# Value projections at 512 moving columns in a decoder trunk: two GLA/stick-breaking mixers re-tiled

## The chip, the cores and the metric

One Trainium2 chip, one core of it. The time is device microseconds (us) of one execution of the whole program; a kernel's time is the median over its runs. The engines are named as in the profile: PE (TensorE matmul), PEld (its weight loads), DVE (VectorE), ACT (ScalarE), POOL (GpSimd), SP (SyncE, which issues the loads of weights).

## The reference

A decoder trunk of two layers on 512 tokens with 1024 features, all in float32. Layer 0 has a gated linear attention (GLA) as its mixer, layer 1 a stick-breaking attention (SB); each mixer stands between two half-step SwiGLU FFNs with 2816 hidden features.

```python
x += 0.5 * swiglu(rmsnorm(x));  x += mixer(rmsnorm(x));  x += 0.5 * swiglu(rmsnorm(x))   # per layer
# GLA: 4 heads, q and k of 128, v and g of 256 features a head
q, k, v, g, gk_lr = split(h @ w_in, [512, 1024, 2048, 3072])
log_a = log_sigmoid(gk_lr @ w_gk2 + b_gk) / 16           # decay of every key feature
o = recurrence(q, k, v, cumsum(log_a))                    # causal, state 128 x 256 a head
out = (rmsnorm(o per head) * silu(g)) @ w_out
# SB: 16 heads of 64 features
q, k, v = split(h @ w_in, 3)
z = q k^T / 8;  w = exp(log_sigmoid(z) - (sum of softplus(z) over later s)), s < t
out = (w @ v) @ w_out
```

The values v are `h @ w_in[:, 1024:2048]` in GLA and `h @ w_in[:, 2048:3072]` in SB. Those two projections are what the change touches.

## The kernel before

All activations stay in the core's memory; every weight is streamed once. A product in float32 accuracy is made of three fp32r matmuls: high part times high part, high times low and low times high. So each weight block is cut by a cast to its high part (`wh`, ACT) and a subtraction to its low part (`wl`, DVE).

**The weight stream.** `Feed` holds a queue of `Entry` objects in the order of use. An entry consists of units (parts of a chunk, 4 KB a partition) and a body, a generator that issues its matmuls and yields after each part; one such part is called a step. A `Chunk` is one load from memory by SP's queue (usually 1 MB). `feed.start()` opens the next entry: it splits the units of up to three entries, so long as no more than four units are held (the pool of `wh` and `wl` has four buffers each), and asks for the loads of up to six. `feed.step(n)` advances by n steps.

**The projections.** `feat` makes 128 features on the partitions with all 512 tokens moving: 24 matmuls of 128x512 in two steps of 12 (`ps_f` in the profile). `tok` makes the values, with tokens on the partitions and weight columns moving (`ps_t`): a call covers 256 columns; for each of four token tiles it issues 24 matmuls of 128x256 into half a PSUM bank, then yields. After every second tile ACT evacuates both halves, each scaled by its tokens' 1/rms (`evac_v`, L691 in GLA and L980 in SB). There are four calls in each mixer, 16 steps, 384 matmuls. PSUM's banks go by tags; tag "a", used by `feat` and `tok` here, has two banks.

**GLA.** `run` first opens the queries, keys, values and gates in the queue. Per head, `levels(h)` builds the decayed score matrix block by block, and `output(h)` transposes keys (`ps_kd`), makes the states (`ps_s`) and the output (`ps_o`), squares it (`osq`), sums over features (`ps_on`), takes 1/rms by the exp and ln tables of ACT (`y`, `vv`) and scales (`on`, L885). A step of the weight stream is put after almost every piece, so that PE has products to do while ACT and DVE work on the chain. At the fourth head the rest of the projections is done, `silu` applies the gates' activation on ACT, and `close` multiplies `on` with the gate and cuts it into `oh` and `ol` for the output projection `back` (`ps_b`).

```python
for n, _ in enumerate(self.levels(h)):
    feed.step(1)
    if prev is not None and n >= 1:
        next(prev, None)          # a part of the previous head's output
        if n == 4:
            feed.step(1)
```

**SB.** The queue holds eight pairs of heads (`pair`: one `feat` for q, one for k) with the four `tok` calls between them. A loop over s = 0..16 makes for head s the logits and their scan (`weights_log`: `ps_z`, softplus on ACT, scan on DVE) and for head s - 1 the weights, transposed (`weights`: `ps_T`, `wt`), and after a pair of heads `values` (`ps_oT`). A list gives the steps of the weight stream for each s.

Of the kernel before, what the change touches and what calls it, by code (L numbers as in the profile page):

```python
# [10 lines left out]
F32 = mybir.dt.float32  # L11
# [19 lines left out]
def decoder(ctx: ExitStack, tc: tile.TileContext, a: dict, out: bass.AP):  # L31
    nc = tc.nc

    # ---------------------------------------------------------------- pools
# [16 lines left out]
    # ------------------------------------------------------------ constants  # L51
# [15 lines left out]
    # --------------------------------------------------------- weight stream  # L67
    # Every weight matrix passes through here in the order of use: chunks of 1 MB are
    # loaded, cut into units of 4 KB a partition, split into high and low parts, and
    # multiplied. An entry is one or more units with the products that use them.  # L70
    class Chunk:
        def __init__(self, src, n, m):
            self.src, self.n, self.m, self.t = src, n, m, None
            self.pool = None
            self.few = False
# [12 lines left out]
    class Entry:  # L88
        """units: (chunk, view of it, n, m); body(W) yields between parts of the products."""

        def __init__(self, units, body):
            self.units, self.body, self.W = units, body, None

        def split(self):
            if self.W is None:
                self.W = []
                for ch, view, n, m in self.units:
                    r = view(ch.load())
                    few = n * m < 1024
                    pool, x, bufs = (st["few"], "v", 1) if few else (wp, "w", 4)  # L100
                    h = pool.tile([P, n, m], F32R, tag=x + "h", bufs=bufs, name="wh")
                    l = pool.tile([P, n, m], F32R, tag=x + "l", bufs=bufs, name="wl")
                    st["cut"] = nc.scalar.copy(h, r).ins  # L103
                    with tc.issue_after(st["gains"]):
                        nc.vector.tensor_tensor(out=l, in0=r, in1=h.bitcast(F32), op=ALU.subtract)  # L105
                    self.W.append((h, l))

    class Feed:
# [3 lines left out]
        def start(self):  # L112
            i = self.pos
            self.pos += 1
            used = 0
            for e in self.q[i : i + 3]:
                used += sum(n * m >= 1024 for _, _, n, m in e.units)
                if used > 4:
                    break
                e.split()  # L120
            for e in self.q[i : i + 6]:
                for u in e.units:
                    u[0].load()
            e = self.q[i]
            return e.body(e.W)

# [26 lines left out]
    def feat(ch, f, evac, tag=None, defer=None):  # L153
        """features f*128.. of a [P, KD, 256] chunk on partitions, all tokens"""
# [16 lines left out]
    def tok(w, c0, evac, tag=None):  # L171
        """columns c0..c0+256 with the tokens on partitions; evac(i, ps[P, 256])"""
        ch = Chunk(cols(w, c0, 256), KD, 256)

        def body(W):
            ps = None
            for i in range(NT):
                if i % 2 == 0:
                    ps = psum("ps_t", tag)
                o = ps[:, (i % 2) * 256 : (i % 2) * 256 + 256]  # L180
                s = slice(i * P, (i + 1) * P)
                for k in range(KD):
# [9 lines left out]
        feed.q.append(  # L192
            Entry([(ch, (lambda t, u=u: t[:, u * 4 : u * 4 + 4]), 4, 256) for u in range(2)], body)
        )
# [66 lines left out]
    def down(w, r0, nf, hs, part, nxt):  # L261
        """x[d] += 0.5 * sum_f w[r0 + f, d] h[f] for the 8 / nf blocks d of a part"""
# [22 lines left out]
    def back_tok(w, r0, nf, hs, done):  # L285
        """the same with tokens on partitions: done(dh, i, ps) gets 512 features of token tile i"""
# [23 lines left out]
    # ----------------------------------------------------------------- norms  # L310
# [24 lines left out]
    def stats_a(tag=None):  # L335
        """r4[token, tile]: 1 / rms of the residual"""
# [23 lines left out]
    def stats_b(tag=None):  # L360
        """R[any partition, token]: the same along the free axis"""
# [11 lines left out]
    def two_halves(between=None):  # L373
        """the next two entries, the first half of both before the second"""
# [20 lines left out]
    def act(o, i, fn, **kw):  # L395
        """an activation of the Exp and Ln tables, queued behind their load"""
        with tc.issue_after(st["tab"]):
            st["last"] = nc.scalar.activation(o, i, fn, **kw).ins

    # ------------------------------------------------------------------- FFN  # L400
    class FFN:
        """The chunks of 256 features go in groups: gate and up, with down for the group
        before between them. From product NORMED on the input is scaled by 1/rms ahead of
        it. The gate's products from chunk SEVEN on, and those of up for the chunks SEVEN_UP,
        go by Winograd's form of Strassen's scheme: seven products of half size for the
        2 x 2 halves of features, inputs and tokens."""
# [5 lines left out]
        def __init__(self, wg, wu, wd, gi, nxt, first=False, last=False):  # L412
# [6 lines left out]
            for group, (c0, c1) in enumerate(self.GROUPS):  # L419
                slots, put = 2 * (c1 - c0), 0  # L420
                for i in range(slots):
# [5 lines left out]
                    if first and c == 0:  # L427
                        # the first products wait for no more of the weights than they need
# [16 lines left out]
                    # the sums are made of the residual as it came  # L445
# [112 lines left out]
        def t_half(self, i, j):  # L558
            """T(i + 1) of input block j"""
# [17 lines left out]
        def normed_input(self):  # L577
            """the scaled input, and T1 = B12 - B11, T2 = B22 - T1, T3 = B22 - B12, T4 = B21 - T2"""
# [21 lines left out]
        def sums(self):  # L600
            def piece(i):
                # in the place of the unscaled input
# [50 lines left out]
    # ------------------------------------------------------------------- GLA  # L653
    class GLA:
        def __init__(self, w_in, w_gk2, b_gk, og, w_out, nxt):
# [13 lines left out]
            for c in range(4):  # L669
                tok(w_in, 1024 + c * 256, lambda i, ps, c=c: self.evac_v(c, i, ps), "a")  # L670
# [235 lines left out]
        def run(self):  # L906
            with ExitStack() as es:
# [20 lines left out]
                for h in range(4):  # L928
# [363 lines left out]
```

## Time and profile before

| | |
|---|---|
| time, median of 3 runs | 1913.95 us (1913.91 to 1914.23) |
| span of the profiled execution | 1913.4 us (it has no time of its own beside it) |
| instructions | 28787 |
| DVE 76%, ACT 49% | 1462.7 us and 943.6 us busy |
| data moved | 179.05 MB, mean 94 GB/s |
| GLA mixer in the trace | about 360 to 595 us |
| SB mixer in the trace | about 1306 to 1554 us |
| 768 value matmuls (ps_t) | 5% of the chain that ended last |

The page gives the busy time of each engine and its share of the span; matmuls are pipelined, so PE's spans overlap and the distance from start to start tells what one costs. The chain of waits is followed back from the last instruction: it tells what released each piece of work. The timeline gives start, duration and, in brackets, the idle time ahead of an instruction and what ended it.

### The profile page before, as it was taken

Reading aid. Unit: us, or ns where it says so; the run is one execution under the profiler, and the core shown is the slowest. Engines: PE = TensorE matmul, PEld = TensorE weight load, DVE = VectorE, ACT = ScalarE, POOL = GpSimd, SP = SyncE. Lnnn points to the kernel's source line nnn. Section 1 sums busy time; section 2 is a strip of 40 time slices with the busy share of each in tenths; the row PEclk is TensorE's granted clock in tenths of the full one; section 3 lists DMA queues with packets and bytes.
Section 4 is the critical chain, followed back from the end, with each engine's and each line's share of the span. In section 5 each row is a group of like instructions: output and inputs, shape, how many; then the busy total and the mean of one; then the engine's idle time right before and its main releaser. Section 6 shows DMA issues by size and latency. Waiting matters only on the chain.

```text
span 1913.4 us, 28787 instructions
## 1 busy us (share of the span) xinstructions
PE 1893.6 (99%) x11789; PEld 1687.9 (88%) x11789; DVE 1462.7 (76%) x2314; ACT 943.6 (49%) x1450; POOL 6.8 (0%) x16
## 2 busy tenths in 40 slices
PE   8999999999999999999999999999999999999998
PEld 7999999889887899999989999998888788899997
DVE  7978777775666977877788778776877779777775
ACT  6534434443554544444453444445878745344444
POOL 0000000100000000000000000000000000000000
PEclk9999999999999999999999999999999999999999
DMA  5423332312123223332233333223221123333321
GB/s 156 144 89 108 103 111 90 96 46 65 60 73 110 89 89 112 105 114 78 78 113 119 100 101 108 79 89 100 66 67 59 63 89 110 99 100 105 116 78 66
DMA packets 177511, 179.05 MB, mean 94 GB/s; under 512 B 3906, under 2 KB 167924, under 8 KB 177380
## 3 DMA queue, kind: packets, MB, share of 16 engines
q1 hardware_dynamic: 176912, 176.24, 29.3%
q8 instruction: 92, 1.51, 0.3%
q0 software_dynamic: 368, 0.95, 0.2%
q14 instruction: 39, 0.32, 0.1%
q10 hardware_dynamic: 100, 0.03, 0.0%
HBM read 175.11 MB, written 2.10 MB: 93 GB/s over the span
## 4 chain that ended last, share of the span: by engine, by line
PE 96%; DVE 2%; DMA 1%; ACT 1%; issue 0%; POOL 0%; SPq 0%; DVEq 0%; POOLq 0%; ACTq 0%
PE ps_d L60 24%; PE ps_f L60 20%; PE ps_w L487 15%; PE ps_z L487 10%; PE ps_q L487 10%; PE ps_t L60 5%; PE ps_b L60 3%; PE ps_S L60 1%; PE ps_z L1019 1%; PE ps_bt L60 1%; PE ps_oT L1081 1%; PE ps_T L1066 1%; PE ps_o L60 1%; DMA x<-in_x_dram 0%; DMA raw<-in_ffn_w_up_dram 0%; DVE wl L105 0%
## 5 line engine op out<-in xcount | busy, mean ns | idle before, releaser
L105 DVE TENSOR_TENSOR wl<-raw,wh 128x1024 fp32r<-128x1024 f32 x244 | 261.4, 1072 | 94.7 <-ACT wh L103 72.8
L103 ACT CAST wh<-raw 128x1024 fp32r<-128x1024 f32 x244 | 226.0, 931 | 142.3 <-PE ps_f L60 44.5
L60 PE MATMUL ps_d<-hh,wh 128*128 128x512 f32 x672 | 262.9, 391 | 0.0
L60 PE MATMUL ps_d<-hh,wl 128*128 128x512 f32 x672 | 262.7, 391 | 0.0
L60 PE MATMUL ps_d<-hl,wh 128*128 128x512 f32 x672 | 262.3, 390 | 0.0
L103 ACT CAST wh<-s 128x1024 fp32r<-128x1024 f32 x136 | 142.7, 1049 | 153.9 <-PE ps_q L487 84.1
L276 DVE SCALAR_TENSOR_TENSOR x<-ps_d,x 128x512 f32<-128x512 f32 x184 | 126.0, 688 | 101.1 <-PE ps_d L60 100.7
L105 DVE TENSOR_TENSOR wl<-s,wh 128x1024 fp32r<-128x1024 f32 x136 | 166.4, 1223 | 32.4 <-ACT wh L103 27.4
L60 PE MATMUL ps_f<-xh,wh 128*128 128x512 f32 x448 | 182.1, 407 | 2.9 <-DVE q L682 1.5
L60 PE MATMUL ps_f<-xl,wh 128*128 128x512 f32 x448 | 175.4, 392 | 0.0
L60 PE MATMUL ps_f<-xh,wl 128*128 128x512 f32 x448 | 175.0, 391 | 0.0
L103 ACT CAST wh<-rawd 128x1024 fp32r<-128x1024 f32 x84 | 88.4, 1052 | 160.1 <-PE ps_d L60 139.2
L487 PE MATMUL ps_z<-th,wl 128*128 128x256 f32 x544 | 154.0, 283 | 0.0
L487 PE MATMUL ps_z<-th,wh 128*128 128x256 f32 x544 | 154.0, 283 | 0.0
L487 PE MATMUL ps_z<-tl,wh 128*128 128x256 f32 x544 | 153.9, 283 | 0.0
L487 PE MATMUL ps_w<-nl,wh 128*128 128x256 f32 x544 | 153.6, 282 | 0.0
L487 PE MATMUL ps_w<-nh,wl 128*128 128x256 f32 x544 | 153.4, 282 | 0.0
L487 PE MATMUL ps_w<-nh,wh 128*128 128x256 f32 x544 | 153.4, 282 | 0.0
L60 PEld LDWEIGHTS ps_d<-hl,wh 128*128 128x128 f32 x672 | 126.1, 188 | 27.6
L60 PEld LDWEIGHTS ps_d<-hh,wh 128*128 128x128 f32 x672 | 126.3, 188 | 25.5
L60 PEld LDWEIGHTS ps_d<-hh,wl 128*128 128x128 f32 x672 | 126.3, 188 | 24.9
L105 DVE TENSOR_TENSOR wl<-rawd,wh 128x1024 fp32r<-128x1024 f32 x84 | 102.9, 1225 | 46.3 <-ACT wh L103 33.4
(246 smaller groups left out, 4725.3 us busy)
## 6 DMA issues: line engine op xcount, KB each, us to landing
raw<-in_ffn_w_gate_dram SPq DMA_DIRECT2D x43, 1024.0 KB, 5.4
raw<-in_ffn_w_up_dram SPq DMA_DIRECT2D x43, 1024.0 KB, 5.3
rawd<-in_ffn_w_down_dram SPq DMA_DIRECT2D x84, 512.0 KB, 3.5
raw<-in_gla_w_in_dram SPq DMA_DIRECT2D x12, 1024.0 KB, 5.3
raw<-in_sb_w_in_dram SPq DMA_DIRECT2D x16, 512.0 KB, 3.9
raw<-in_gla_w_out_dram SPq DMA_DIRECT2D x4, 1024.0 KB, 5.0
raw<-in_sb_w_in_dram SPq DMA_DIRECT2D x4, 1024.0 KB, 5.1
raw<-in_sb_w_out_dram SPq DMA_DIRECT2D x4, 1024.0 KB, 5.1
```

Of the source, the lines that this page charges most:

```text
L60: nc.tensor.matmul(ps, l, r, start=first, stop=last)
L103: st["cut"] = nc.scalar.copy(h, r).ins
L105: nc.vector.tensor_tensor(out=l, in0=r, in1=h.bitcast(F32), op=ALU.subtract)
L276: nc.vector.scalar_tensor_tensor(out=xs[k], in0=ps, scalar=0.5, in1=xs[k], op0=ALU.mult, op1=ALU.add)
L487: nc.tensor.matmul(o, l_, r_, start=first and j + n == 0, stop=j == 3 and n == 2, skip_group_check=True)
L1019: nc.tensor.matmul(o_, l_, r_, start=first, stop=last, skip_group_check=True)
L1066: nc.tensor.transpose(ps[:, c0 : c0 + P], ys[yb][:, yc + j * P : yc + (j + 1) * P], ident)
L1081: nc.tensor.matmul(po[e * 64 : e * 64 + 64, j * P : T], self.v[j][:, c : c + 64], self.wt[p, e][bk][:, c0 : c0 + n], start=j == 0, stop=j ...
```

## The change

`tok` covers 512 columns a call, in two calls for each mixer. Its weights are four units of 2 blocks x 512 columns (two chunks of 4 blocks x 512, 1 MB each). The four token tiles go in two pairs; a pair holds two PSUM banks, walks the four units, and yields after each unit: 12 matmuls of 128x512 a step, 8 steps a call, 16 steps a mixer as before. Each tile is evacuated by one instruction of 128x512 at the pair's last unit. `Entry.split` can ready a part of an entry's units, `Feed.start` hands out what is left of the four, `ahead` readies one more unit at each step of the second pair, and `loads` asks for loads while no more than two chunks of a kind are unsplit.

Around it, GLA makes its additional step in the second head also at n = 3, so that one step less is left for the fourth. In SB the values' second half comes after pair 4 (it was in four quarters after pairs 0, 2, 4 and 6), six steps are made ahead of the loop instead of four, and the first two heads get two steps each instead of three. FFNs are not edited.

```diff
     def tok(w, c0, evac, tag=None):
-        ch = Chunk(cols(w, c0, 256), KD, 256)
+        units = []
+        for k0 in range(0, KD, 4):
+            ch = Chunk(w[k0 * P : k0 * P + 512, c0 : c0 + 512].rearrange("(k p) c -> p k c", p=P), 4, 512)
+            for u in range(0, 4, 2):
+                units.append((ch, (lambda t, u=u: t[:, u : u + 2]), 2, 512))
         def body(W):
-            ps = None
-            for i in range(NT):
-                if i % 2 == 0:
-                    ps = psum("ps_t", tag)
-                o = ps[:, (i % 2) * 256 : (i % 2) * 256 + 256]
-                s = slice(i * P, (i + 1) * P)
-                for k in range(KD):
-                    wh, wl = W[k // 4]
-                    mm(o, st["h"][k][:, s], wh[:, k % 4], k == 0, False)
-                    mm(o, st["h"][k][:, s], wl[:, k % 4], False, False)
-                    mm(o, st["l"][k][:, s], wh[:, k % 4], False, k == KD - 1)
-                if i % 2:
-                    evac(i - 1, ps[:, 0:256])
-                    evac(i, o)
-                yield
+            for pair in ((0, 1), (2, 3)):
+                ps = [psum("ps_t", tag) for _ in pair]
+                for u in range(4):
+                    wh, wl = W[u]
+                    for n, i in enumerate(pair):
+                        s = slice(i * P, (i + 1) * P)
+                        for kk in range(2):
+                            k = 2 * u + kk
+                            mm(ps[n], st["h"][k][:, s], wh[:, kk], k == 0, False)
+                            mm(ps[n], st["h"][k][:, s], wl[:, kk], False, False)
+                            mm(ps[n], st["l"][k][:, s], wh[:, kk], False, k == KD - 1)
+                        if u == 3:
+                            evac(i, ps[n])
+                    if pair[0]:
+                        feed.ahead()
+                    yield
...
 class Feed, start():
             for e in self.q[i : i + 3]:
-                used += sum(n * m >= 1024 for _, _, n, m in e.units)
-                if used > 4:
+                n = sum(n * m >= 1024 for _, _, n, m in e.units)
+                e.split(4 - used if n else 1)
+                used += n
+                if used >= 4 and n:
                     break
-                e.split()
-            for e in self.q[i : i + 6]:
-                for u in e.units:
-                    u[0].load()
+            self.loads(i)
...
+        def ahead(self):
+            for e in self.q[self.pos : self.pos + 4]:
+                if not e.whole():
+                    e.split(1)
+                    self.loads(self.pos)
+                    return
...
 class GLA:
-            for c in range(4):
-                tok(w_in, 1024 + c * 256, lambda i, ps, c=c: self.evac_v(c, i, ps), "a")
+            for c in range(2):
+                tok(w_in, 1024 + c * 512, lambda i, ps, c=c: self.evac_v(c, i, ps), "a")
...
-                            if n == 4:
+                            if n == 4 or n == 3 and h == 1:
                                 feed.step(1)
...
 class SB:
-            pair(0), vals(0), pair(1), pair(2), vals(1), pair(3), pair(4), vals(2)
-            pair(5), pair(6), vals(3), pair(7)
+            pair(0), vals(0), pair(1), pair(2), pair(3), pair(4), vals(1)
+            pair(5), pair(6), pair(7)
...
-                feed.step(4)
-                steps = [3] * 12 + [2, 1, 1, 2, 2]
+                feed.step(6)
+                steps = [2, 2] + [3] * 10 + [2, 1, 1, 2, 2]
```

More of the change, by code (lines that the diff above doesn't have):

```diff
@@ L73, in __init__ @@
             self.src, self.n, self.m, self.t = src, n, m, None
+            self.left = 0
             self.pool = None
@@ L91, in __init__, with whole, split @@
         def __init__(self, units, body):
[L92 to L106, printed above, removed]
+            self.units, self.body, self.W = units, body, []
+            for u in units:
+                u[0].left += 1
+        def whole(self):
+            return len(self.W) == len(self.units)
+        def split(self, parts=4):
+            for ch, view, n, m in self.units[len(self.W) :][:parts]:
+                r = view(ch.load())
+                ch.left -= 1
+                few = n * m < 1024
+                pool, x, bufs = (st["few"], "v", 1) if few else (wp, "w", 4)
+                h = pool.tile([P, n, m], F32R, tag=x + "h", bufs=bufs, name="wh")
+                l = pool.tile([P, n, m], F32R, tag=x + "l", bufs=bufs, name="wl")
+                st["cut"] = nc.scalar.copy(h, r).ins
+                with tc.issue_after(st["gains"]):
+                    nc.vector.tensor_tensor(out=l, in0=r, in1=h.bitcast(F32), op=ALU.subtract)
+                self.W.append((h, l))
     class Feed:
@@ L116, in start, with loads @@
             for e in self.q[i : i + 3]:
-                used += sum(n * m >= 1024 for _, _, n, m in e.units)
-                if used > 4:
+                n = sum(n * m >= 1024 for _, _, n, m in e.units)
+                e.split(4 - used if n else 1)
+                used += n
+                if used >= 4 and n:
                     break
-                e.split()
-            for e in self.q[i : i + 6]:
-                for u in e.units:
-                    u[0].load()
+            self.loads(i)
             e = self.q[i]
             return e.body(e.W)
+        def loads(self, i):
+            seen, held = set(), {False: 0, True: 0}
+            for e in self.q[i : i + 6]:
+                for ch, _, _, _ in e.units:
+                    if id(ch) in seen:
+                        continue
+                    seen.add(id(ch))
+                    if ch.left and ch.pool is None:
+                        held[ch.few] += 1
+                        if held[ch.few] > 2:
+                            return
+                    ch.load()
+        def ahead(self):
[3 more added lines that the diff above has]
+                    self.loads(self.pos)
+                    return
         def step(self, n=1):
@@ L171, in tok @@
     def tok(w, c0, evac, tag=None):
[L173 to L194 removed]
+        units = []
[3 more added lines that the diff above has]
+                units.append((ch, (lambda t, u=u: t[:, u : u + 2]), 2, 512))
+        def body(W):
+            for pair in ((0, 1), (2, 3)):
[14 more added lines that the diff above has]
+                    yield
+        feed.q.append(Entry(units, body))
     def back(w, r0, nf, hs, scale, nxt, late=0, tags=(None,) * 8):
@@ L691, in evac_v @@
             nc.scalar.activation(
[L692 removed]
+                self.v[i][:, c * 512 : c * 512 + 512], ps, AF.Copy, scale=st["r4"][:, i : i + 1]
             )
```

5 lines of the change are left out of this document (2 added, 3 removed).

## The prediction

> **What bounds the kernel now.** I read the page first: busy shares, clock row, and the shares of the chain that ended last.
>
> ```profile
> PE 1893.6 (99%) x11789; PEld 1687.9 (88%) x11789; DVE 1462.7 (76%) x2314; ACT 943.6 (49%) x1450; POOL 6.8 (0%) x16
> PEclk9999999999999999999999999999999999999999
> PE 96%; DVE 2%; DMA 1%; ACT 1%; issue 0%; POOL 0%; SPq 0%; DVEq 0%; POOLq 0%; ACTq 0%
> ```
>
> TensorE (PE) is busy 99% of the span and 96% of the chain. So time can only come from PE's own work or from its idle time, and the view of waits, PE alone, says how much idle time there is.
>
> ```profile
> PE ps_g L1210 <- DMA gl<-in_gla_o_norm_dram: 5.8, 1, 5.8
> PE ps_f L60 <- DVE q L682: 1.5, 1, 1.5
> PE ps_x L1217 <- DMA x<-in_x_dram: 1.4, 4, 0.7
> PE ps_f L60 <- DVE x L211: 1.4, 1, 1.4
> PE ps_o L60 <- DVE on L885: 0.7, 1, 0.7
> PE ps_b L60 <- ACT oh L902: 0.5, 1, 0.5
> ```
>
> Together 11.3 us, 7.2 of it on the first loads. No wait on a weight's load stands here, and only 0.7 + 0.5 = 1.2 us lie inside the mixers' hand-made weaves (ps_o, ps_b); what else there is are single waits of 0.2. The edit can therefore gain from cheaper matmuls, and lose wherever it takes cover from an ACT or DVE chain. The span is 1913.4 us and the median of the runs 1913.95; the 0.55 us between them I keep constant. The profiled execution has no time of its own beside its span.
>
> **Term 1, the matmuls: a gain.** Half of the columns per matmul becomes full width: 768 of 256 become 384 of 512, that is 32 steps of 24 become 32 steps of 12. The chain of waits, pieces in order (start, us, what), has both widths in both mixers.
>
> ```profile
> 455.56 2.93 PE ps_t L60 x24
> 497.02 2.82 PE ps_f L60 x12
> 1317.36 5.87 PE ps_t L60 x48
> 1329.87 5.47 PE ps_f L60 x24
> 1361.12 2.87 PE ps_t L60 x24
> 1350.00 2.77 PE ps_f L60 x12
> 1837.35 2.82 PE ps_w L487 x24
> 1848.72 5.59 PE ps_d L60 x24
> ```
>
> ps_t is the value projection at 256 columns, ps_f a projection at 512 with the same products. One step surrounded by other work costs 2.93 against 2.82 in GLA and 2.87 against 2.77 in the stick-breaking mixer (SB): 0.10 to 0.11 saved. Two steps in a row give 5.87 against 5.47, 0.20 a step. In the last FFN 24 narrow ones take 2.82 and 12 wide ones 5.59/2 = 2.795: only 0.025. So 32 steps save between 0.8 and 6.4 us. Most steps lie among other work, like the first and third pair of rows, a few follow one another; I take 0.12, 3.8 us.
>
> [...]
>
> **Term 2, the end of GLA: a loss.** The extra step at `n == 3 and h == 1` takes a step of 12 ps_f matmuls from the place before the fourth head's output, where they cover a serial chain. Before, PE ran 30 ps_f after the third ps_on; the changed order has 19 (11 fewer), then three ps_kd, then one ps_o ahead of twelve ps_b. Here is the timeline (start, duration, engine; rows of PE, then ACT, then DVE).
>
> ```profile
> 549.03 1.12 PE L60 MATMUL ps_on<-osq,ones 128*128 128x512 f32 x2
> 557.89 0.50 PE L60 MATMUL ps_b<-oh,wh 128*128 128x512 f32 x1 [0.55 <-ACT oh L902]
> 560.65 1.21 PE L60 MATMUL ps_o<-S,v 128*128 128x128 f32 x6 [0.65 <-DVE on L885]
> ...
> 550.92 0.63 ACT L398 ACTIVATE y<-vv 128x512 f32<-128x512 f32 x1 [2.08 <-DVE vv L871]
> 551.58 1.28 ACT L398 ACT_TABLE_LOAD   x1
> 553.30 0.62 ACT L398 ACTIVATE y<-y 128x512 f32<-128x512 f32 x1
> 555.76 0.61 ACT L878 ACTIVATE y<-y 128x512 f32<-128x512 f32 x1
> 556.28 1.04 ACT L103 CAST wh<-raw 128x1024 fp32r<-128x1024 f32 x1
> 557.23 1.13 ACT L902 CAST oh<-on 128x512 fp32r<-128x512 f32 x2
> ...
> 556.41 0.69 DVE L879 TENSOR_TENSOR vv<-vv,y 128x512 f32<-128x512 f32 x1 [2.43 <-ACT y L878]
> 557.66 0.42 DVE L880 TENSOR_SCALAR vv<-vv 128x512 f32<-128x512 f32 x1
> 557.99 1.22 DVE L105 TENSOR_TENSOR wl<-raw,wh 128x1024 fp32r<-128x1024 f32 x1
> 559.85 1.41 DVE L885 SCALAR_TENSOR_TENSOR on<-ps_o,gT,y 128x512 f32<-128x512 f32 x2
> ```
>
> I walk the changed order with these durations, from ps_on = 0; an engine's next instruction starts some 0.1 before the former's end, as 556.28 does against 555.76 + 0.61. PE: two ps_on 1.12 / 2 = 0.6 ahead of the next start, 19 ps_f at 2.82 / 12 = 0.235, ps_kd: done at 5.4. ACT: y (ln) starts at 1.9 as here, table load until 3.8, y's exp until 4.9, y's square until 5.4, then the cast wh until 6.4. There oh followed; in the changed order the next table load (1.28) and the gate's silu (as wide as y: 0.6) stand behind the cast and are followed by one more load (1.28), so that oh starts at 9.6. DVE: vv by y until 6.1, wl until 7.6 (it waits for wh), vv 0.4, y by vv 0.7, and the two on, done at 9.4 and 10.0. ps_o needs the bank that on reads and starts near 9.4, ps_b with the first oh near 10.1, and its third product waits a little more for ol. PE idles 4.7 us where it idled 1.2: +3.5 us. Bounds: +1.5 if only the shorter cover counts, 11 x 0.235 = 2.6, less the 1.2 that a chain without the load ahead of y's square comes earlier; +4.5 if the second on and all of ol are needed before anything runs. The step itself isn't lost: it runs in the second head, where PE has no wait that it could fill.
>
> **Terms 3 and 4, SB: losses.** Steps of SB are rebalanced: six instead of four run before the scan loop, and the first two heads get 2 each instead of 3. Windows (busy us of PE, PEld, DVE, ACT in turn):
>
> ```profile
> 1317.00:1335.00 18.00, 18.00 (x132) 17.08 (x132) 11.96 (x24) 9.58 (x14) 0.00 (x0) 1.00 0.32 94
> 1335.00:1345.00 10.00, 10.00 (x49) 8.08 (x48) 7.60 (x12) 9.14 (x18) 0.00 (x0) 1.00 0.32 95
> 1345.00:1356.00 11.00, 11.00 (x59) 8.80 (x58) 10.77 (x17) 9.00 (x18) 0.00 (x0) 1.00 0.17 50
> 1381.00:1406.00 25.00, 25.00 (x134) 19.39 (x132) 21.55 (x33) 21.05 (x41) 0.00 (x0) 1.00 0.23 69
> 1481.00:1505.00 24.00, 23.39 (x126) 16.83 (x124) 20.08 (x31) 22.45 (x49) 0.00 (x0) 1.00 0.27 88
> ```
>
> The two heads of the first pair are the second and third rows: 21.0 us of PE over ACT 18.1 and DVE 18.4. Two steps less leave PE 21.0 - 2 x 2.77 = 15.5 us, while ACT keeps nearly all its work, since pair 1's scaling and casts now run there whole, just ahead of their use, where before a pair stood between. PE is then short by at most 18.1 - 15.5 = 2.6 us by ACT and 2.9 by DVE. In front, in the first row, ACT has 8 us of 18 free and takes some of it, the casts of the two steps' units (1.04 each) to begin with: I take 1.7, bounds 0 and 2.9.
>
> Values' second half now lies after pair 4 and before pair 5, so pair 5's K too is made just before use, once, and by one head: half of the above, +0.8 (0 to 1.5). In stretches of projections only (fourth row) ACT and DVE have 4 us of 25 to spare, in the tail (fifth row) ACT has 1.5 of 24 and PE already lost 0.61; that is why such a place costs anything.
>
> **What I cost at nothing.** Evacuations: 32 of 128x256 become 16 of 128x512. From
>
> ```profile
> L691 ACT ACTIVATE v<-ps_t,r 128x256 f32<-128x256 f32 x16 | 6.8, 469 | 9.0 <-PE ps_t L60 8.9
> ```
>
> and 0.63 for a 512-wide ACTIVATE (550.92, above), ACT saves 32 x 0.47 - 16 x 0.63 = 5 us in all; ACT is off the path at those places, so nothing is gained. In exchange a pair of tiles holds both banks of tag "a" until its last step, and the next group waits for both evacuations: 0.63 and 1.26 us behind the last matmul. The other tag's step (2.8 us) usually stands between; if that cover is gone it costs up to 1 us at each of the pairs' ends, four places in GLA, which I keep in the range. Weights: units are cut one ahead at a time in the second pair; a unit serves 24 wide matmuls, over 5 us, its cut is one wh (1.04) and one wl (1.22). The loads on SP's queue keep their order and their bytes, with rows twice as long, and no wait on them stood in the list of waits. FFN keeps its order but for a few exchanged neighbours on DVE. The 1.4 us stall on x L211 shifts along unchanged.
>
> **Sum.** -3.8 + 3.5 + 1.7 + 0.8 = +2.2 us: span 1915.6, time 1916.1 (1913.95 + 2.2).
>
> **Rivals.** (a) The gain comes through: the steps save 0.20 each as the two in a row do, 6.4 us, SB's covers hold (ACT did have 4 us to spare in 25), and GLA's end costs 2.5: -3.9, 1910.0. Against it: single steps showed 0.10. (b) Slower: in the long stretch of projections without values, pairs 2, 3 and 4 come just in time as well, not only 1 and 5. Each costs the mean of 1.7 and 0.8, together +3.8: 1919.9. It decides where the last ps_f of a pair's K ends less than some 2 us (scaling, cast and remainder in series, each about the 0.63 to 0.69 of the 512-wide rows above) before its first ps_z. For it speaks DVE's 21.55 of 25; against it that the loop still gives three steps a head there.
>
> (c) The clock falls in GLA's stall. At the kernel's start, after sparse work, ps_f start 0.42 apart until 18.39 and 0.23 from there, although the clock row above is full; the first one behind the 1.39 us stall lasts 0.50, hardly more than usual.
>
> ```profile
> 17.55 0.63 PE L60 MATMUL ps_f<-xl,wh 128*128 128x512 f32 x1
> 18.39 0.39 PE L60 MATMUL ps_f<-xh,wl 128*128 128x512 f32 x1
> 18.62 0.40 PE L60 MATMUL ps_f<-xl,wh 128*128 128x512 f32 x1
> 612.06 0.50 PE L60 MATMUL ps_f<-xh,wh 128*128 128x512 f32 x1 [1.39 <-DVE x L211]
> ```
>
> My 4.7 us of idle lies between those cases. The start's seven or so slow matmuls at 0.2 extra each cost 1.4 us: 1917.5. [...] No row of this trace tells whether a 4 us stall is enough.
>
> (d) The wide matmuls gain only what the last FFN shows, 0.8: +5.2, 1919.1. (e) The change does not do what it says, the two banks held by a pair making PE wait as much as the width saves: near 1914.
>
> **How the numbers follow.** Forecast 0.44, (a) 0.18, (b) 0.16, (c) 0.10, (d) 0.06, (e) 0.06. About 0.2%, 3.8 us, is what a measurement of this kernel can tell from no change, so the bounds are 1910.1 and 1917.8. Faster: nearly all of (a) and a little of the forecast with its low bounds, 0.18. Slower: (b), (d), a part of (c) and the forecast's upper bounds, 0.31. Same: 0.51. The range reaches from (a)'s 1909.8 to a little beyond (b), 1920.4; the forecast's own, with half of each term's spread, is 1913.5 to 1918.5.
>
> **What would show it.** Right: ps_t 128x512 pieces of 12 at 2.77 to 2.82 in the chain; new PE waits near GLA's end on DVE on and ACT oh of 4 to 5 us together; waits of ps_T, ps_z on ACT wt, kh and DVE kl at SB's first pair and at pair 5. Wrong: GLA's wait under 2 us, PE waits at pairs 2 to 4, waits of ps_t or the next group on the evacuations, or pieces of 12 over 2.9.

## The result, and the profile after

| | before | changed |
|---|---|---|
| time, median of 11 runs | 1914.23 us (1913.91 to 1915.09) | 1918.92 us (1918.08 to 1919.53) |
| ratio | | 1.0023 (95% interval 1.0015 to 1.0032) |
| span of the profiled execution | 1913.4 us | 1916.1 us (its time: 1918.08) |

The change costs 4.7 us, 0.24%, and no run of the changed kernel is as fast as the slowest of before. In every later run of both kernels the time is 1.7 to 2.2 us above the span. So the profiled execution of before, with its span of 1913.4, was one of about 1915.3 us and not one at the median; most of what it has too much lies in the first loads, and the two spans differ by only 2.7 us. The comparison is therefore made stage by stage.

The page, PE's busy time and the chain's shares:

```profile
PE 1892.2 (99%) x11405; PEld 1668.2 (87%) x11405; DVE 1461.4 (76%) x2314; ACT 941.3 (49%) x1434; POOL 6.8 (0%) x16
PE 94%; DVE 3%; ACT 2%; DMA 1%; issue 0%; DVEq 0%; ACTq 0%; SPq 0%
```

PE has 384 instructions less. Its busy share is the same 99%, but its share of the chain falls from 96% to 94%, and DVE's and ACT's rise. The view of waits, PE alone, says where:

```profile
PE ps_o L60 <- DVE on L916: 4.1, 1, 4.1
PE ps_T L1097 <- ACT wt L429: 1.9, 2, 1.4
PE ps_f L60 <- DVE q L713: 1.5, 1, 1.5
PE ps_x L1248 <- DMA x<-in_x_dram: 0.6, 3, 0.3
PE ps_z L1050 <- DVE kl L1037: 0.6, 2, 0.3
PE ps_z L1050 <- DVE kh L1035: 0.3, 1, 0.3
```

Against the same view of before: ps_o waits 4.1 instead of 0.7, ps_b's 0.5 is gone, ps_T, kl and kh are new, and the 1.4 on x at the second FFN's start is missing. The chain of waits has the wide pieces themselves:

```profile
456.25 2.82 PE ps_t L60 x12
1316.54 5.62 PE ps_t L60 x24
1411.25 2.77 PE ps_t L60 x12
```

2.93, 5.87 and 2.87 have become 2.82, 5.62 and 2.77: the width pays 0.10 to 0.13 a step at these places, where the forecast took 0.12. Now the end of GLA. The timeline (start, duration; PE, then ACT, then DVE):

```profile
557.91 0.77 PE L60 MATMUL ps_o<-S,v 128*128 128x128 f32 x2 [4.13 <-DVE on L916]
558.45 0.80 PE L60 MATMUL ps_b<-oh,wh 128*128 128x512 f32 x1
559.04 0.63 PE L60 MATMUL ps_b<-oh,wl 128*128 128x512 f32 x1
559.47 0.63 PE L60 MATMUL ps_b<-ol,wh 128*128 128x512 f32 x1
...
561.69 0.39 PE L60 MATMUL ps_b<-ol,wh 128*128 128x512 f32 x1
...
553.49 1.04 ACT L108 CAST wh<-raw 128x1024 fp32r<-128x1024 f32 x1
554.55 1.28 ACT L925 ACT_TABLE_LOAD   x1
555.85 0.63 ACT L925 ACTIVATE gn<-gn 128x512 f32<-128x512 f32 x1
556.49 1.28 ACT L424 ACT_TABLE_LOAD   x1
557.78 2.18 ACT L933 CAST oh<-on 128x512 fp32r<-128x512 f32 x4
...
554.70 1.22 DVE L110 TENSOR_TENSOR wl<-raw,wh 128x1024 fp32r<-128x1024 f32 x1
557.02 1.41 DVE L916 SCALAR_TENSOR_TENSOR on<-ps_o,gT,y 128x512 f32<-128x512 f32 x2
```

The chain of cast, table load, gate, table load and oh on ACT, and of wl, vv, y and on on DVE, runs as the prediction walked it. Behind the idle time the first products start 0.43 us apart; from 561.47 on it is 0.23 again, and their duration falls from 0.63 to 0.39. The windows around them, with the granted clock as the third number from the end, say why:

```profile
556.00:559.00 3.00, 1.08 (x3) 1.00 (x4) 2.93 (x5) 2.98 (x5) 0.00 (x0) 0.81 0.58 177
559.00:561.00 2.00, 2.00 (x6) 1.53 (x5) 2.00 (x5) 1.33 (x3) 0.00 (x0) 0.50 0.70 267
561.00:563.00 2.00, 2.00 (x10) 1.62 (x9) 1.91 (x4) 1.22 (x2) 0.00 (x0) 0.93 0.00 0
```

The granted clock stands at 0.50 in the middle row. If it is 0.50 or full at any moment, which is an assumption, the three rows make 3.4 us of low clock in all (an estimate). Rival (c) has come about, on top of the forecast. In SB the timeline shows five waits that before does not have, three at the first pair, one at pair 5, one in the tail:

```profile
1355.12 0.44 PE L1097 MATMUL ps_T<-ident,r 128*128 128x128 f32 x2 [0.59 <-ACT wt L429]
1357.66 0.53 PE L1050 MATMUL ps_z<-kh,mq 128*128 128x384 f32 x2 [0.27 <-DVE kh L1035]
1359.92 0.44 PE L1050 MATMUL ps_z<-kl,mq 128*128 128x384 f32 x1 [0.32 <-DVE kl L1037]
1461.12 0.44 PE L1050 MATMUL ps_z<-kl,mq 128*128 128x384 f32 x1 [0.24 <-DVE kl L1037]
1491.12 0.44 PE L1097 MATMUL ps_T<-ident,r 128*128 128x128 f32 x2 [1.36 <-ACT wt L429]
```

Between the starts of PE's rows that bound the stages, each from one profiled execution (us; the last four kernels are experiments below; ps_st and ps_R are the small products that make a block's 1/rms, and each head of GLA has one ps_on, each pair of heads in SB one ps_oT):

| stage | before | changed | e1 | e6 | e10 | e12 |
|---|---|---|---|---|---|---|
| start to GLA's ps_R | 378.95 | 377.70 | 377.53 | 378.17 | 376.85 | 378.21 |
| ps_R to the third ps_on | 170.08 | 170.38 | 168.09 | 168.06 | 168.05 | 168.04 |
| third to fourth ps_on | 31.22 | 32.53 | 32.06 | 33.42 | 33.66 | 31.04 |
| fourth ps_on to the second FFN's ps_st | 37.61 | 36.42 | 36.30 | 36.28 | 36.28 | 36.48 |
| ps_st to SB's ps_R | 705.20 | 704.96 | 704.96 | 705.21 | 704.97 | 704.97 |
| SB's ps_R to the first ps_oT | 44.39 | 45.62 | 45.64 | 44.41 | 44.16 | 43.67 |
| first to last ps_oT | 155.55 | 158.05 | 158.03 | 155.39 | 156.45 | 156.46 |
| rest | 390.40 | 390.44 | 390.39 | 390.46 | 390.48 | 390.43 |

Without the first row, which holds the first loads, changed less before is +0.30 + 1.31 - 1.19 - 0.24 + 1.23 + 2.50 + 0.04 = +3.95 us. The profiled execution of the changed kernel is its fastest; its median lies 0.8 higher.

### The profile page after: what moved, and what is told of

Read it like the earlier page. It is cut to its first block, busy times and chain, and to the rows that moved or that the text cites. A ratio compares the mean times of both kernels' runs of the same rounds, so it can differ in the third digit from the quotient of the medians.

```text
span 1916.1 us, 28001 instructions
## 1 busy us (share of the span) xinstructions
PE 1892.2 (99%) x11405; PEld 1668.2 (87%) x11405; DVE 1461.4 (76%) x2314; ACT 941.3 (49%) x1434; POOL 6.8 (0%) x16
## 3 DMA queue, kind: packets, MB, share of 16 engines
q8 instruction: 89, 1.46, 0.3%
## 4 chain that ended last, share of the span: by engine, by line
PE 94%; DVE 3%; ACT 2%; DMA 1%; issue 0%; DVEq 0%; ACTq 0%; SPq 0%
PE ps_d L60 24%; PE ps_f L60 19%; PE ps_w L518 15%; PE ps_z L518 10%; PE ps_q L518 10%; PE ps_t L60 5%; PE ps_b L60 3%; PE ps_S L60 1%; PE ps_bt L60 1%; PE ps_oT L1112 1%; PE ps_z L1050 1%; PE ps_o L60 1%; PE ps_T L1097 1%; DVE l L1075 1%; ACT l L429 0%; DVE wl L110 0%
```

## The experiments

Theory: the wide products gain about 4 us, GLA's end loses it in idle time and half clock, SB loses as much again at single places of its weave. Main rival: the wide form with its two held banks costs the time itself. "Against before" is always against runs of the kernel before on the same chip.

### e1: who pays for GLA's additional step

```diff
-                            if n == 4 or n == 3 and h == 1:
+                            if n == 4 and h != 2 or n == 3 and h == 1:
```

> The changed kernel, but GLA's additional step at n == 3 of the second head is paid by the third head (its own additional step at n == 4 is left out) and no longer by the end: 30 instead of 19 ps_f again between the third ps_on and ps_kd. My theory (the changed kernel's +4.7 us against before is -4.2 of cheaper matmuls, +2.9 of PE idle at GLA's end, +1.4 of products at half clock behind that idle time, and some +3.5 in SB, less 1.2 at the second FFN's start): the 4.1 us wait of ps_o and the slow ps_b go, 4.3 us; the second FFN's start may wait its 1.2 us for a load again; so +0.4 to +1.6 against before. Rival (the wide matmuls and the two banks that a pair holds cost the time themselves, the place of the step nothing): +4 to +5 as now.

Measured: 1915.46 us against 1913.94, +1.52; ratio 1.0008 (0.9999 to 1.0017). The view of waits:

```profile
PE ps_o L60 <- DVE on L916: 1.5, 1, 1.5
PE ps_b L60 <- ACT oh L933: 0.7, 1, 0.7
PE ps_T L1097 <- ACT wt L429: 2.0, 2, 1.4
```

4.1 has become 1.5 + 0.7, and 3.2 of the 4.7 us are back. By the code the step is needed in the second head (the state products there read values of all four token tiles, which the wide form completes four steps later than quarters did); a kernel without it was not run. The third head can pay for it, the end of the mixer can't. In the table, ps_R to the third ps_on with equal numbers of steps: 170.08 - 168.09 = 2.0 us for 16 wide steps, 0.125 each. The changed kernel has one step more in this stretch, which costs 170.38 - 168.09 = 2.3 us. The wait at the second FFN's start did not return.

### e2: SB's list of steps as before

```diff
-                feed.step(6)
-                steps = [2, 2] + [3] * 10 + [2, 1, 1, 2, 2]
+                feed.step(4)
+                steps = [3] * 12 + [2, 1, 1, 2, 2]
```

> The changed kernel with SB's list of steps as before (four ahead of the loop, three in each of the first two heads); the values keep their new places. My theory: the three waits at the first pair (0.59, 0.27 and 0.32) go, the wait of 1.36 in the tail stays: -1.0 us against the changed kernel, +3.7 against before. Rival (the waits come from the values' places, not the list): within 0.3 of the changed kernel, +4.7.

Measured: 1918.75 us against 1913.94, +4.81; ratio 1.0024 (1.0015 to 1.0033). A miss: the rival was right. Two waits went and others came (ps_z on r 0.9 in three places), and from SB's ps_R to the first ps_oT it takes 45.79 us where the changed kernel takes 45.62. The list is not the cause.

This run's profile also shows a longer stretch of half clock in a GLA that is the same program:

```profile
556.00:559.00 3.00, 1.49 (x4) 1.24 (x5) 2.96 (x5) 2.98 (x6) 0.00 (x0) 0.60 0.78 240
559.00:561.00 2.00, 2.00 (x6) 1.60 (x6) 2.00 (x4) 0.92 (x3) 0.00 (x0) 0.50 0.46 172
561.00:563.00 2.00, 2.00 (x6) 1.51 (x6) 1.92 (x4) 1.22 (x2) 0.00 (x0) 0.50 0.00 0
```

The next window, 563 to 566, still has 0.93, so by the same estimate the clock is low for 6.8 us where it was 3.4 above, and the third to the fourth ps_on takes 33.70 us instead of 32.53. Such a difference, 1.2 us, could be most of the spread of 1.5 us between the changed kernel's runs: the granted clock on record is 0.998 in the five fastest of its eleven runs and 0.997 in four of the six others. Other causes of the spread were not separated.

### e4: the new weave alone, with 256 columns

```diff
 (kernel before)
-            pair(0), vals(0), pair(1), pair(2), vals(1), pair(3), pair(4), vals(2)
-            pair(5), pair(6), vals(3), pair(7)
+            pair(0), vals(0), vals(1), pair(1), pair(2), pair(3), pair(4), vals(2), vals(3)
+            pair(5), pair(6), pair(7)
 (the values' first two calls take banks of tag "z", before only the first)
-                            if n == 4:
+                            if n == 4 or n == 3 and h == 1:
-                feed.step(4)
-                steps = [3] * 12 + [2, 1, 1, 2, 2]
+                feed.step(6)
+                steps = [2, 2] + [3] * 10 + [2, 1, 1, 2, 2]
```

> The kernel before, its value projections in calls of 256 columns, with only the weave of the changed kernel: the additional step at n == 3 of the second head, SB's calls two after pair 0 and two after pair 4, six steps ahead of the loop and two in each of the first two heads. My theory: it pays for the weave without the gain of the width: +4.7 + 4.2, about +9 (+7.5 if a part of the waits shrinks since each narrow step covers 0.13 more). Rival (the weave costs nothing, the wide form does): 0 to +1.

Measured: 1922.62 us against 1913.94, +8.68; ratio 1.0044 (1.0032 to 1.0057). The same waits stand in it:

```profile
PE ps_o L60 <- DVE on L885: 4.1, 1, 4.1
PE ps_T L1066 <- ACT wt L398: 1.4, 1, 1.4
```

So the weave costs 8.7 us with narrow values, and the changed kernel is 8.68 - 4.69 = 4.0 us faster than that. The rival that the wide form costs the time is ruled out. But the 4.0 us are not 0.125 for each of 32 steps. Stage by stage, e4 against the changed kernel, GLA up to the third ps_on takes 172.38 and 170.38 us, 2.0 for its 16 steps; the second FFN's start gives 0.8, which comes from a load (see "At nothing" below) and not from the width; and SB with the FFNs ahead of it takes 705.22 + 46.28 + 158.00 and 704.96 + 45.62 + 158.05, only 0.9 for the other 16. The changed kernel pays about 1 us there at a place that e4 does not have (e9).

### e5: the idle time cut in two

```diff
 (GLA.output, behind vv = 1.5 - 0.5 vv y y)
+            if h == 2:
+                mm(psum("ps_x", "z"), ones, vv, True, True)
```

> The changed kernel with one extra product of 128x512 (ones by vv, the result unused) that becomes ready in the middle of the idle time at GLA's end and cuts the 4.1 us in two. My theory (half clock because PE was idle for some 4 us at one stretch): the granted clock stays at 1.0 there, the twelve ps_b behind it start 0.23 apart instead of 0.43, -1.4 us, so +3.3 against before. Rival (those products are slow because their operand ol comes one by one from DVE): no change of the rate, +4.7 or a little more.

Measured: 1917.17 us against 1913.94, +3.23; ratio 1.0016 (1.0007 to 1.0025). The timeline:

```profile
556.05 1.10 PE L60 MATMUL ps_x<-vv,ones 128*128 128x512 f32 x2 [2.62 <-DVE vv L911]
557.57 0.68 PE L60 MATMUL ps_o<-S,v 128*128 128x128 f32 x4 [0.42 <-DVE on L918]
558.10 0.50 PE L60 MATMUL ps_b<-oh,wh 128*128 128x512 f32 x1
558.44 0.40 PE L60 MATMUL ps_b<-oh,wl 128*128 128x512 f32 x1
```

More work, less time: the products behind the gap last 0.40 and not 0.63, and the third to the fourth ps_on takes 31.07 us, 1.46 less. The granted clock is 1.00 in each window from 553 to 566. They were slow because of the idle time, not because of ol: PE's order is a little different here, with products of oh ahead of those of ol, but e10 has that order too, and with the low clock (0.55 in its window from 557 to 560) they start 0.43 apart in it.

### e6: GLA wide, SB as before

The edit: e1, with SB's four calls of 256 columns, their order and the list of steps from the kernel before.

> GLA as in e1 (512 columns, the step paid by the third head), SB wholly as before (four calls of 256 columns, their places and the list of steps). My theory (losses in SB come from the values' places, and the stages add up): GLA and the second FFN's start keep e1's 236.5 us where before has 238.9, SB returns to before's: -2.5 us against before, 1911.4. Rival (a part of SB's loss is carried into it, or GLA's gain is given back later): +0 to +1.5 like e1.

Measured: 1912.37 us against 1913.84, -1.47; ratio 0.9993 (0.9984 to 1.0001). SB returns to 44.41 and 155.39, so the stages add up, and its losses are made by SB itself. One us of the expected 2.5 is missing, and in the profiled execution a window in GLA shows a place for it, with a granted clock of 0.60:

```profile
557.00:560.00 3.00, 2.28 (x9) 1.71 (x8) 3.00 (x6) 2.99 (x6) 0.00 (x0) 0.60 0.40 78
```

The low clock also stood behind the smaller gaps of 1.5 and 0.7 us, but not in every execution: e1's and e9's profiles, with the same GLA, have a granted clock of 1.00 from 557 to 566 and take 32.06 and 32.05 us from the third to the fourth ps_on, those of e6, e7, e8 and e10 have 0.81 in that stretch and take 33.42 to 33.66.

### e7: pair 1 ahead of the values

```diff
 (e1)
-            pair(0), vals(0), pair(1), pair(2), pair(3), pair(4), vals(1)
+            pair(0), pair(1), vals(0), pair(2), pair(3), pair(4), vals(1)
 (pair 1 takes banks of tag "z", its q is evacuated when R is there; the values take "a")
```

> e1 with pair 1's q and k projected ahead of the values' first half (their banks exchanged with the values'), so that they lie a whole group before their use. My theory (the first pair's waits of 0.60, 0.27 and 0.35 come from K made just before use): they go, -1.2 to -2.0 against e1, -0.5 to +0.3 against before. Rival (ACT and DVE are short of time in the first two heads whatever the order): the waits stay in another form, within 0.4 of e1.

Measured: 1913.64 us against 1913.84, -0.20; ratio 1.0000 (0.9991 to 1.0008). The three waits of the first pair are gone; in its list ps_T and kl keep one wait each, those of the tail and of pair 5:

```profile
PE ps_T L1097 <- ACT wt L429: 1.4, 1, 1.4
PE ps_z L1050 <- DVE kl L1037: 0.2, 1, 0.2
```

From the first ps_z to the first ps_oT 26.45 us instead of e1's 28.42, 2.0 less. So what hurt was that all eight steps of values lie ahead of pair 1, whose K is then made just before use.

### e8: the second half in quarters

```diff
 (e1; quarter(c) is the narrow call of before)
-            pair(0), vals(0), pair(1), pair(2), pair(3), pair(4), vals(1)
-            pair(5), pair(6), pair(7)
+            pair(0), vals(0), pair(1), pair(2), pair(3), pair(4), quarter(2)
+            pair(5), pair(6), quarter(3), pair(7)
```

> e1 with the values' first half at 512 columns and the second half in two calls of 256, after pairs 4 and 6, as before. My theory (the wait of 1.36 in the tail, the cut ps_oT and the late kl come from pairs 5, 6 and 7 standing in a row at the end, since the whole second half lies ahead of them): from the first to the last ps_oT 155.5 to 155.8 us as before, not 158.0: -2.3 against e1, -0.8 against before. Rival (the tail's wait is a delay handed on from the first pair): 1.36 stays, within 0.5 of e1.

Measured: 1913.12 us against 1913.84, -0.72; ratio 0.9996 (0.9987 to 1.0005). From the first to the last ps_oT 155.88 us, not 158.03, and the wait of 1.36 is gone, though the waits at the first pair are as in e1. The tail's wait is therefore its own, and it comes from the place and not from the width, as e4 has 1.36 there with narrow values: with quarter(3) between pairs 6 and 7, ACT and DVE get four steps without casts of q and k.

### e9: the second half after pair 5

```diff
 (e1)
-            pair(0), vals(0), pair(1), pair(2), pair(3), pair(4), vals(1)
-            pair(5), pair(6), pair(7)
+            pair(0), vals(0), pair(1), pair(2), pair(3), pair(4), pair(5), vals(1)
+            pair(6), pair(7)
```

> e1 with the values' second half, 512 columns, after pair 5 instead of pair 4. My theory: pair 5's late kl (0.22) and the cut ps_oT between pairs 3 and 5 go, which gives 0.8 to 1.3, the tail's wait of 1.36 stays as pairs 6 and 7 still stand in a row: +0.2 to +0.8 against before. Rival (the values are then late for pair 4's ps_oT, since they end only one head ahead of it): a new wait there, +1.5 or more.

Measured: 1913.35 us against 1913.84, -0.49; ratio 0.9997 (0.9989 to 1.0006), a miss on the good side of +0.2 to +0.8. First to last ps_oT 156.34 us, 1.7 less than e1, with a wait of 1.5 in the tail as foreseen. Between the third and the fifth ps_oT it takes 24.48 + 24.48 us, e1 21.73 + 29.08: there the changed order cuts pair 3's ps_oT in two with a step between, as in this timeline of the changed kernel:

```profile
1439.08 1.07 PE L1112 MATMUL ps_oT<-wt,w 128*64 128x512 f32 x2
1440.08 0.50 PE L60 MATMUL ps_f<-xh,wh 128*128 128x512 f32 x1
...
1443.07 2.37 PE L1112 MATMUL ps_oT<-wt,w 128*64 128x512 f32 x14
```

1.00 + 2.30 us to the next start, where the uncut sixteen take 1419.65 - 1417.35 = 2.30 at the pair before in the same trace: about 1 us without any idle time in the list of waits. e4, which does not cut it, takes 25.04 + 25.10 us over the same twelve steps, less than the changed kernel's 21.73 + 29.11 although five of them are narrow. An edit that moves the cut alone was not tried.

### e10: both moves together

The edit: e7's and e9's orders in one kernel, all values wide.

> e7 and e9 together: all values at 512 columns, the step paid by GLA's third head, pair 1 ahead of the values' first half, the second half after pair 5. My theory (SB's losses are single places and add up): from ps_R of SB to the last ps_oT 17.2 + 26.5 + 156.3 = 200.0 us, as before has 199.9 and e1 203.7; GLA keeps e1's gain, less what half clock takes in some executions; -1.5 against before, as e6. Rival (the moves exclude each other, a wait goes from one place to the next): 202 us and more, +0.5.

Measured: 1911.76 us against 1913.89, -2.13; ratio 0.9990 (0.9982 to 0.9999). SB takes 44.16 + 156.45 = 200.6 us; e1 203.7, before 199.9. The moves add up; of the waits that before does not have, SB keeps the tail's, 1.5, and 0.3 at the first pair.

### e11: still more cover at GLA's end

```diff
 (e6)
-                            if n == 4 and h != 2 or n == 3 and h == 1:
+                            if n == 4 and h < 2 or n == 3 and h == 1:
```

> e6 (GLA at 512 columns, SB as before) with the fourth head's additional step left out as well: 42 ps_f between the third ps_on and ps_kd instead of 30. My theory (what is left to lose in GLA is PE's idle time of 1.5 + 0.7 us at its end, and half clock behind it in some executions): the wait of ps_o falls below 1 us, the granted clock stays at 1.0, the heads before lose nothing; -1.9 against e6, -3.3 against before. Rival (the step was cover in the fourth head, its chain then waits there): new waits between the heads' ps_kd and ps_on of 1 us and more, -1.5 or worse.

Measured: 1912.17 us against 1913.89, -1.72; ratio 0.9990 (0.9981 to 0.9999). A miss: 0.25 better than e6 where 1.9 was expected. One line of waits and the timeline of ACT:

```profile
PE ps_b L60 <- ACT oh L958: 2.4, 1, 2.4
...
553.29 1.05 ACT L108 CAST wh<-raw 128x1024 fp32r<-128x1024 f32 x1 [2.44 <-PE ps_f L60]
554.24 0.63 ACT L950 ACTIVATE gn<-gn 128x512 f32<-128x512 f32 x1
554.87 1.28 ACT L449 ACT_TABLE_LOAD   x1
556.16 2.18 ACT L958 CAST oh<-on 128x512 fp32r<-128x512 f32 x4
```

ps_o no longer waits, but ps_b does. The steps put there make the last gate, and oh stands behind that gate's activation and a table load on ACT: the cover moves the end of the chain it is to cover. This execution, the second fastest of eleven, has the full clock behind the 2.4 us (1.00 in each window from 557 to 566); the median is 1.3 us longer, and whether the low clock came in the other runs is not shown.

### e12: both moves, and the idle time broken

The edit: e10 with e5's two lines.

> e10 with e5's extra product (ones by vv, its result unused) in GLA's remaining idle time of 1.5 + 0.7 us. My theory (also 2.2 us of idle time, of which 1.5 at a stretch, brings half clock in some executions and costs them 1.3 us): the granted clock stays at 1.0 in all of them, the slower half of e10's runs goes: 0.6 less in the median, -2.7 against before, and a spread below 1.2 us. Rival (the spread of e10's runs has another cause, such as the kernel's first loads): median and spread as e10, -2.1.

Measured: 1910.90 us against 1914.45, -3.55; ratio 0.9982 (0.9973 to 0.9991); spread 1.18 us against e10's 2.24. The windows of e10 and e12 at the same place, in this order:

```profile
557.00:560.00 3.00, 3.00 (x9) 2.33 (x9) 3.00 (x6) 2.17 (x5) 0.00 (x0) 0.55 0.72 259
```

```profile
557.00:560.00 3.00, 2.95 (x13) 2.44 (x14) 2.63 (x4) 2.98 (x5) 0.00 (x0) 1.00 0.37 58
```

The granted clock stays full, 1.00, and the third to the fourth ps_on takes 31.04 us. This is the best of all: 3.6 us faster than before, 8 faster than the change as it was made. But the product did more than break the idle time. In PE's order it stands ahead of the last ps_f, and of the waits of 1.5 and 0.7 us only 0.13 is left: on ACT, oh now comes ahead of the last gate and of a table load that it stood behind in e10.

```profile
556.38 1.14 ACT L935 CAST oh<-on 128x512 fp32r<-128x512 f32 x2
557.42 0.63 ACT L927 ACTIVATE gn<-gn 128x512 f32<-128x512 f32 x1
558.06 1.28 ACT L424 ACT_TABLE_LOAD   x1
```

e1 and e9 have the two waits at full clock and take 32.06 and 32.05 us, 1.0 more than e12. So a part of the gain is the new order's and not the clock's; how the 1.4 us between the medians of e10 and e12 divide was not tried.

## Why the prediction was right or wrong

The forecast was 1916.1 us with 1909.8 to 1920.4 around it, and a rise too small to tell from none. Measured were 1918.92 and +4.7: inside the wide range, but twice the forecast's +2.2, just outside the forecast's own 1913.5 to 1918.5, and a little beyond the bound of 0.2%, so "slower" (0.31) came and not "same" (0.51). What lies between forecast and result are terms of the sum and the rival (c), less a load and a remainder that nobody forecast. That the time lies near (d)'s 1919.1 is chance, since GLA's steps save 0.125 each and not 0.025.

**Term 1** (-3.8): right in GLA, where 16 steps save 2.0 us (e1, e4), 0.125 each with 0.12 forecast. Two of SB's steps stand in the row from ps_st to SB's ps_R, which takes 705.21 us with narrow values (before, e6) and 704.96 with wide ones, again 0.125 each and not the 0.20 that the row of two steps had suggested. The other fourteen were not separated from the weave; e4's 4.0 us agree with -3.8 only because they hold 0.8 of a load and lack what the cut ps_oT takes.

**Term 2** (+3.5): the place, the chain and the order were right. PE idles 4.13 us instead of 1.20, +2.9 where +3.5 was forecast: ps_b does not wait a second time, since oh came while ps_o ran. What failed is that the sum stopped at the idle time. In the other direction, the moved step is not neutral: it costs 2.3 us ahead of the third ps_on (e1) and leaves about 3.1 at the end (2.93 of idle time and 1.46 of low clock, less the 1.31 by which that stage grew), 0.8 in its favour. Why was not tried.

**Rival (c)** had 0.10 and was priced at 1.4: it is no rival but part of term 2. It took 1.46 us (e5) in one pair of profiled executions, 1.2 more in e2's, and was there in the profile of each kernel that has the 4.1 us at a stretch. The granted clock was 0.50 in a window behind those 4.13 us in the changed kernel, in e2 and in e4, and 1.00 throughout in e5, whose longest stretch is 2.62, and in e11 behind 2.36. But the longest stretch alone does not tell the cases apart: behind gaps of 1.5 and 0.7 with 1.3 us of small products between them the clock was low in some executions (0.60 in e6 and 0.55 in e10 from 557 to 560) and 1.00 in others (e1, e9). What decides it, and what ends the low clock, was not shown.

**Term 3** (+1.7, in the first two heads): the size was right, the cause was wrong. From ps_R to the first ps_oT there are thirteen steps in each kernel, of which before has five narrow ones, the changed kernel none and e4 six. At 0.125 a step, the losses without the width are 1.23 + 0.6 and 1.89 - 0.1: 1.8 to 1.9 us. But the prediction put it on the list's two steps in place of three; e2 gives them back and gains nothing, e7 moves pair 1 and gains 2.0. The step that failed is "two steps less leave PE" short: with either list twelve steps lie ahead of pair 1's first ps_z (2 + 6 + 2 + 2 or 2 + 4 + 3 + 3), the eight of values first and then the four of pair 1, so that its K comes no earlier.

**Term 4** (+0.8, at pair 5): the mis-sized one. First to last ps_oT takes 2.5 us more, in the changed kernel and in e4. Before has nine narrow steps there, the changed kernel none and e4 eight, so without the width the losses are 2.5 + 1.1 = 3.6 and 2.45 + 0.1 = 2.6. The kl of pair 5 did wait, 0.24; 1.36 came in the tail, where pairs 6 and 7 now stand in a row behind pair 5 (e8 takes it away), and about 1 at the cut ps_oT, which e4 does not have (e9). About 1 us in both stays open. The prediction looked for the price where values had been put in, and not where they had been taken out. This is rival (b)'s mechanism, but at pairs 6 and 7 and not at 2 to 4.

**At nothing**: the evacuations, the held banks, the single cuts and the FFNs cost nothing that a wait shows. The 1.4 us on x at the second FFN did not shift along, it went, and the stage is 1.2 us shorter. The chain of waits has a load of the FFN's weights (raw from in_ffn_w_up) ahead of that x, which the view of PE's own waits does not name, as PE waits for it through ACT and DVE: 6.56 us before, 5.26 in the changed kernel. In e4, with the feed of before, it took 6.07, in e5 and e12 5.22 and 5.32. What makes the load shorter was not tried.

**The base**: "0.55 us between span and median" was wrong. The time lies 1.7 to 2.2 us above the span in every run, so that the span shown belonged to a slower execution. The sum was not hurt, as it went from the median.

Sum of the pieces as measured: GLA +1.6 (-2.0 of width, +2.9 idle, +1.5 low clock, -0.8 of the moved step), the load -1.2, SB +3.5 (e4's weave 4.35, less the 0.9 by which the changed kernel is faster there) = +3.9, and 0.8 from the profiled to the median execution: 4.7, as measured. That the miss is no larger is in part luck: the low clock and SB's later stretch were missing or too small in the forecast, and the load and the moved step, which were not in it either, go the other way.

## What to carry to other kernels

In this kernel, with PE busy for 99% of the span, the wider tile was worth 0.125 us a step where it could be measured alone, close to the 0.10 to 0.11 that single steps had shown before, and the price was in the weave: a coarser unit must be done earlier, and the steps for that are taken from some other place, where the profile has to be asked what they had covered. When a block of work without casts is moved, look also at the place it leaves, since there the work that loads ACT and DVE now stands in a row (here a wait of 1.36 us, which e8 takes away). Cover is only cover if the chain does not end behind it (e11, where ps_b then waits 2.4 us).

## What the runs showed of the hardware

The gap of 4.13 us on PE cost about 1.5 us more than itself in the changed kernel's profiled execution (32.53 us from the third to the fourth ps_on against 31.07 in e5), as matmuls behind it started 0.43 instead of 0.23 us apart at a granted clock of 0.50; by the estimate from the windows the clock was low for 3.4 us in one execution and 6.8 us in another (e2). One product of 128x512 with an unused result in the gap saved that 1.5 us in e5, where the time from the first ps_kd to ps_o stays 4.62 us, the longest idle stretch falls to 2.62 and the granted clock is 1.00. The spread between runs fell from 2.24 to 1.18 us with it in e12, but in e5 it is 1.65 against the changed kernel's 1.45. The same low clock after gaps of 1.5 and 0.7 us, in four of six profiles with this GLA (0.81 against 1.00 from 557 to 566), was not expected.
